# A decoder step on one core: the second layer's pooled products as three fp32r products of halves, 47 to 50 blocks later

## The chip, the cores and the metric

The kernel runs on 1 core of one Trainium2 chip. What is measured is the device time of one execution in microseconds (us); the number given is the median over the runs. Smaller is better. The engines that matter here are TensorE (PE: matmuls and weight loads), VectorE (DVE), ScalarE (ACT), GpSimd (POOL) and SyncE (SP, which issues most DMAs).

## The reference

Two layers of a decoder are computed for 256 prompt rows and 8 sample rows together (T = 264 columns). The second layer has two heads side by side: stick-breaking attention, and a pooling mixer that the change touches. The mixer takes running means of its input `u` over windows of 2, 4, 8 and 16 rows, subtracts `u`, multiplies each of the four 128-wide groups by a 128x128 matrix, and scales the result:

```python
pooled = jnp.concatenate(parts, axis=-1) - u_new.astype(jnp.float32)
pooled = pooled.astype(u_new.dtype).reshape(B, T, POOL_GROUPS, POOL_GROUP_DIM)
mixed = jnp.einsum('btgc,gcd->btgd', pooled, pool_w).reshape(B, T, D_WIDTH)
return mixed * pool_scale
```

Attention output and mixer output are then concatenated and multiplied by `w_out`:

```python
c_out = stick_breaking_attention(q, k_all, v_all, pos).reshape(B, T, C_WIDTH)
d_out = pool_mixer(pool_prev, u, pos, pool_w, pool_scale)
y = jnp.concatenate([c_out, d_out], axis=-1) @ w_out
return x + y, new_kv, new_pool
```

After it come a residual, a feed-forward part with a short convolution, and at the very end a norm.

## The kernel before

**Blocks.** All large weights pass through TensorE as 1472 blocks of 128x128 in a fixed order (`_PHASES`): in0, out0, ff0, dn0 for the first layer, in1, out1, ff1, dn1 for the second. A block is three fp32r matmuls over 264 columns, since each weight and each operand is cut into a high and a low half: high by high, low operand by high weight, high operand by low weight (L329 to L331). The halves of the weights are made eight blocks at a time (a tile): ScalarE writes the high half `wh` (L304), VectorE the low half `wl` (L305), three tiles ahead of use, in four buffers each.

**in1 and out1.** Phase in1 has 128 blocks: blocks 1 to 32 make `u`, 33 to 64 `q`, 65 to 96 `k`, 97 to 128 `v`, eight blocks for each 128 output rows. The accumulators are called after the block number over the whole kernel: `mm848`, `mm856`, `mm864`, `mm872` are the four of `v` (blocks 97, 105, 113 and 121 of in1), `mm880` is the first of out1. out1 starts with its k rows 4 to 7, which are the mixer's output `catB`, before it comes to the attention's output `catA` (`kb` in `_phases`).

**Hooks.** `blk(b, f)` calls f after block b of the phase. In in1 TensorE is held in program order (`fixed[0] = True`), so a hook's matmuls stand exactly after that block. The order on VectorE and ScalarE is made when the program is built, by a scheduler with its own model of times; on the chip each engine then works its list strictly in that order. The hooks of in1 that matter: the pooled sums at 33 (`pool_sum`), the pooled products at 62, 66, 70 and 76 (`pool_mix`), the sample scores at 72 (`zs_score`), the four scores of head pairs at 80, 93, 105 and 117 (`z_qk`, two matmuls each for `Z`; then `stick`: three sigmoids on ScalarE, a scan and a product on VectorE, for each head), and the transposes of `w` and `v` at 117 (`z_tr`, `v_turn`).

**Banks.** PSUM is split into two pools of four banks. The pool `psm` (tag "mm", function `mmb`) gives the banks of the block accumulators, of the pooled products `pm`, and of the transposes `vtp_v` of `v`. Which free bank a new tile takes is settled when the program is built; its first matmul waits until the instruction that empties that bank has run: for `v` that is `v.tensor_tensor(v4[:, t, :], o, R, ALU.mult)` in `in1_evac` (L1098), for `pm` the two instructions that write `catB_h` and `catB_l` (L1088, L1089).

**The pooled product before.** `pool_mix(t)` is one fp32 matmul of 128x128 by 128x264, which the chip runs as two instructions, and the two instructions that scale it and cut it into the halves `catB_h` (ScalarE) and `catB_l` (VectorE).

Of the kernel before, what the change touches and what calls it, by code (L numbers as in the profile page):

```python
# [9 lines left out]
F32 = mybir.dt.float32  # L10
F32R = mybir.dt.float32r
BF16 = mybir.dt.bfloat16
I32 = mybir.dt.int32
AF = mybir.ActivationFunctionType
ALU = mybir.AluOpType
# [3 lines left out]
P = 128  # L19
# [4 lines left out]
T = SEQ + NS  # L24
# [182 lines left out]
def tile_decoder_step(ctx: ExitStack, tc: tile.TileContext, a):  # L207
    nc = tc.nc
    v, s, g = nc.vector, nc.scalar, nc.gpsimd
# [14 lines left out]
    pe = TensorE()  # L224
# [10 lines left out]
    def f4(name, shape=(P, 4, T), dt=F32):  # L235
        return up.tile(list(shape), dt, tag="u", name=name)

    def mv(name):
        return [f4(f"{name}_{x}", (P, 4, TW), F32R) for x in "hl"]
# [4 lines left out]
    def at(name):  # L244
        return psa.tile([P, 512], F32, tag="at", name=name)
# [10 lines left out]
    def mmb(name):  # L256

        return psm.tile([P, 512], F32, tag="mm", name=name)

    def vec(n):  # L260
        o, w = _VEC[n]
        return VEC[:, o:o + w]
# [109 lines left out]
    pw = at("warm")  # L372
# [527 lines left out]
    blk = lambda b, f, *x: hk.at(b / 8 - 1, f, *x)  # L900
# [73 lines left out]
    pw = f4("pw", (P, 4, P))  # L974
# [3 lines left out]
    st1 = {}  # L978
# [82 lines left out]
    pl = f4("pl")  # L1061
# [5 lines left out]
    def pool_sum():  # L1067
# [3 lines left out]
        for t, W in enumerate(POOLW):  # L1071
# [8 lines left out]
            v.tensor_reduce(ss, PALL[:, t, :, 16 - W:16], AX.X, ALU.add)  # L1080
            v.scalar_tensor_tensor(pl[:, t, SEQ:T], ss, 1.0 / W, PALL[:, t, :, NST], ALU.mult, ALU.subtract)

    def pool_mix(t):
        pm = mmb(f"pm{t}")
        pe.matmul(pm[:, :T], pw[:, t, :], pl[:, t, :], start=True, stop=True)
        hh, ll = catB[0][:, t, :T], catB[1][:, t, :T]
        gs = vec("ps")[:, t:t + 1]
        s.activation(hh, pm[:, :T], AF.Copy, scale=gs)  # L1088
        v.scalar_tensor_tensor(ll, pm[:, :T], gs, hh.bitcast(F32), ALU.mult, ALU.subtract)  # L1089
# [12 lines left out]
    blk = lambda b, f, *x: hk.at(b / 8 - 1, f, *x)  # L1102
# [10 lines left out]
    blk(84, late, a["poolp"], plp)  # L1113
    blk(84, late, a["pools"], PALL)
    blk(112, late, a["k1"], k4)
    for i, b in enumerate((62, 66, 70, 76)):
        blk(b, pool_mix, i)
    blk(117, lambda: v_turn(vt, v4, range(0, 2), "v1", mmb))
    blk(107, lambda: sample_av(st1, PZ, vtiles, "l1"))
# [52 lines left out]
    for i, (h, m, e) in enumerate(YD):  # L1172
        n = TG[h][1] - TG[h][0]
        y = f4(f"yo{i}", (P, e - m, n))
        w = r[:, TF:] if i == 2 else ns[h][:, HV[h]]
# [74 lines left out]
```

## Time and profile before

| | |
|---|---|
| median of 3 runs | 591.30 us (591.25 to 591.41) |
| the profiled execution | 591.39 us, of which the span of the core is 589.6 us |
| mean granted TensorE clock | 0.998 |
| TensorE busy in the span | 582.4 us (99%) |
| TensorE weight loads | 567.0 us (96%) |
| VectorE busy | 428.8 us (73%) |
| ScalarE busy | 338.2 us (57%) |
| DMA | 122.42 MB, 208 GB/s on average |

The page divides the span by engine, then in 40 slices, then by DMA queue, then follows the chain of waits back from the last instruction, then groups the instructions. Here the chain is TensorE's to 99%. Matmuls overlap in the pipe, so the duration of one in the trace (0.28 us) is more than its share of the time; the distance from one start to the next is what a matmul costs. in1 lies at 300.5 to 362.6 us, the pooled products at 323.5 to 334 us.

### The profile page before, as it was taken

To read this page: it belongs to the slowest core of one execution; us is meant where nothing else is said; L and a number is where in the kernel's file an instruction comes from. 1 tells how busy PE (TensorE), PEld (TensorE's weight loads), DVE (VectorE), ACT (ScalarE), POOL (GpSimd) and SP (SyncE) were. 2 spreads that over 40 slices of the span, in tenths; PEclk is the share of its full clock that TensorE was granted. 3 is DMA by queue.
4 is the path that set the end of the run, shared out by engine and by line. 5 is a ranking of instruction groups with operands and counts; after the bars stand their busy time and mean duration, and the time that the engine had idled before them with its cause. 6 is when DMAs were issued, how large, how long until landed. Compare 5 with 4: busy or idle time off the path is not lost.

```text
span 589.6 us, 12426 instructions
## 1 busy us (share of the span) xinstructions
PE 582.4 (99%) x4972; PEld 567.0 (96%) x4972; DVE 428.8 (73%) x771; ACT 338.2 (57%) x597; POOL 45.2 (8%) x62
## 2 busy tenths in 40 slices
PE   9999999999999999999999999999999999999995
PEld 8999879999999999999999879999999999999995
DVE  6999876787877877566669675778787777756552
ACT  7749746665655655544454556567565565555431
POOL 1000213200000000011030000120000000002111
PEclk9999999999999999999999999999999999999999
DMA  8998764564545455894558772554554546464501
GB/s 349 408 394 294 248 224 166 187 206 157 210 152 206 163 196 178 314 346 170 199 208 288 240 237 89 182 202 170 190 186 172 200 158 215 149 218 154 205 1 73
DMA packets 27564, 122.42 MB, mean 208 GB/s; under 512 B 3314, under 2 KB 4338, under 8 KB 16114
## 3 DMA queue, kind: packets, MB, share of 16 engines
q1 hardware_dynamic: 27072, 120.75, 57.5%
q8 instruction: 39, 0.64, 0.4%
q10 hardware_dynamic: 434, 0.87, 0.4%
q14 instruction: 19, 0.16, 0.1%
HBM read 117.65 MB, written 3.96 MB: 206 GB/s over the span
## 4 chain that ended last, share of the span: by engine, by line
PE 99%; issue 0%; POOLq 0%; DVE 0%; ACT 0%
PE mm L219 91%; PE sc L219 1%; PE pv_l L219 1%; PE pav L219 1%; PE warm L219 1%; PE Z L219 1%; PE S L219 1%; PE pt L222 1%; PE pf L219 0%; PE pm L219 0%; POOLq L1225 0%; PE vtp_v L222 0%; PE ns_n L219 0%; PE po_l L222 0%; PE vtp_sgu L222 0%
## 5 line engine op out<-in xcount | busy, mean ns | idle before, releaser
L304 ACT ACTIVATE wh<-raw 128x1024 fp32r<-128x1024 f32 x177 | 187.3, 1060 | 197.1 <-PE mm L219 186.3
L305 DVE TENSOR_TENSOR wl<-raw,wh 128x1024 fp32r<-128x1024 f32 x177 | 217.1, 1227 | 104.5 <-ACT wh L304 103.9
L219 PE MATMUL mm<-xg_f_h,wh 128*128 128x264 f32 x704 | 199.9, 284 | 0.0
L219 PE MATMUL mm<-xg_f_h,wl 128*128 128x264 f32 x704 | 199.8, 284 | 0.0
L219 PE MATMUL mm<-xg_f_l,wh 128*128 128x264 f32 x704 | 198.6, 282 | 0.0
L219 PEld LDWEIGHTS mm<-xg_f_l,wh 128*128 128x128 f32 x704 | 132.8, 189 | 0.0
L219 PEld LDWEIGHTS mm<-xg_f_h,wh 128*128 128x128 f32 x704 | 132.5, 188 | 0.0
L219 PEld LDWEIGHTS mm<-xg_f_h,wl 128*128 128x128 f32 x704 | 132.4, 188 | 0.0
L219 PE MATMUL mm<-a_h,wl 128*128 128x264 f32 x352 | 100.0, 284 | 0.0
L219 PE MATMUL mm<-a_h,wh 128*128 128x264 f32 x352 | 100.0, 284 | 0.0
L219 PE MATMUL mm<-a_l,wh 128*128 128x264 f32 x352 | 99.7, 284 | 0.0
L219 PEld LDWEIGHTS mm<-a_l,wh 128*128 128x128 f32 x352 | 66.4, 189 | 0.0
L219 PEld LDWEIGHTS mm<-a_h,wh 128*128 128x128 f32 x352 | 66.2, 188 | 0.0
L219 PEld LDWEIGHTS mm<-a_h,wl 128*128 128x128 f32 x352 | 66.2, 188 | 0.0
L219 PE MATMUL mm<-xg_h,wh 128*128 128x264 f32 x160 | 47.1, 294 | 0.0
L219 PE MATMUL mm<-xg_l,wh 128*128 128x264 f32 x160 | 46.0, 287 | 0.0
L219 PE MATMUL mm<-xg_h,wl 128*128 128x264 f32 x160 | 45.9, 287 | 0.0
L219 PE MATMUL mm<-xg_n_h,wh 128*128 128x264 f32 x128 | 38.0, 297 | 0.0
L219 PE MATMUL mm<-xg_n_h,wl 128*128 128x264 f32 x128 | 36.4, 285 | 0.0
L219 PE MATMUL mm<-xg_n_l,wh 128*128 128x264 f32 x128 | 36.3, 284 | 0.0
L219 PEld LDWEIGHTS mm<-xg_h,wh 128*128 128x128 f32 x160 | 30.6, 191 | 1.5 <-issue 1.2
L219 PEld LDWEIGHTS mm<-xg_l,wh 128*128 128x128 f32 x160 | 30.6, 191 | 0.2 <-DVE xg_l L388 0.2
(261 smaller groups left out, 843.4 us busy)
## 6 DMA issues: line engine op xcount, KB each, us to landing
raw<-in_w SPq DMA_DIRECT2D x89, 1024.0 KB, 4.8
K<-in_kt SPq DMA_DIRECT2D x32, 256.0 KB, 6.4
V<-in_vp SPq DMA_DIRECT2D x32, 256.0 KB, 6.6
raw<-in_w SPq DMA_DIRECT2D x4, 512.0 KB, 6.9
X<-in_x SPq DMA_DIRECT2D x4, 264.0 KB, 6.3
xw<-in_xw SPq DMA_DIRECT2D x2, 388.0 KB, 5.3
out_y<-yo SPq DMA_DIRECT2D x2, 300.0 KB, 2.6
out_k<-k SPq DMA_DIRECT2D x1, 528.0 KB, 6.0
```

The lines of the kernel that those rows point to most:

```text
L219: return self.keep(nc.tensor.matmul(*x, **k))
L222: return self.keep(nc.tensor.transpose(*x, **k))
L304: s.activation(h, src, AF.Copy)
L305: v.tensor_tensor(l, src, h.bitcast(F32), ALU.subtract)
```

## The change

A new hook after block 74, `pool_cut`, cuts the pooled sums `pl` (128 x 4 x 264) and the four matrices `pw` (128 x 512) into high and low halves: two instructions on ScalarE, two on VectorE. `pool_mix` then makes each product by three fp32r matmuls of halves (high by high, low operand, low weight) in place of one fp32 matmul, and its hooks move from blocks 62, 66, 70, 76 to 110, 113, 120, 123. The scaling and cutting of the product is as it was. Three more tiles of the general SBUF pool (24 buffers) are taken, for the halves.

```diff
@@ -1080,9 +1080,19 @@
+    def pool_cut():
+        st1["pw"] = f4("pwr", (P, 2, 4, P), F32R)
+        st1["pl"] = mv("plr")
+        for src, h, l in ((pw, st1["pw"][:, 0], st1["pw"][:, 1]), (pl, *(i[:, :, :T] for i in st1["pl"]))):
+            s.activation(h, src, AF.Copy)
+            v.tensor_tensor(l, src, h.bitcast(F32), ALU.subtract)
+
     def pool_mix(t):
         pm = mmb(f"pm{t}")
-        pe.matmul(pm[:, :T], pw[:, t, :], pl[:, t, :], start=True, stop=True)
+        w = [st1["pw"][:, i, t, :] for i in range(2)]
+        x = [i[:, t, :T] for i in st1["pl"]]
+        for i, j in ((0, 0), (0, 1), (1, 0)):
+            pe.matmul(pm[:, :T], w[i], x[j], start=i + j == 0, stop=i == 1)
         hh, ll = catB[0][:, t, :T], catB[1][:, t, :T]
         gs = vec("ps")[:, t:t + 1]
         s.activation(hh, pm[:, :T], AF.Copy, scale=gs)
@@ -1113,7 +1123,8 @@
     blk(84, late, a["poolp"], plp)
     blk(84, late, a["pools"], PALL)
     blk(112, late, a["k1"], k4)
-    for i, b in enumerate((62, 66, 70, 76)):
+    blk(74, pool_cut)
+    for i, b in enumerate((110, 113, 120, 123)):
         blk(b, pool_mix, i)
     blk(117, lambda: v_turn(vt, v4, range(0, 2), "v1", mmb))
     blk(107, lambda: sample_av(st1, PZ, vtiles, "l1"))
```

**TensorE from block 120 of in1 into out1.** What stands there before: `mm864` is the third accumulator of `v`, `mm872` the fourth, `mm880` the first of out1; a name in brackets is the engine whose count the instruction waits for.

```order
L219 MATMUL mm864_4824<-xg_n11_h_1798,wl108_4637 128x264
L219 MATMUL mm872_4904<-xg_n10_h_1796,wh109_4704 128x264
L219 MATMUL mm872_4904<-xg_n10_l_1797,wh109_4704 128x264
L219 MATMUL mm872_4904<-xg_n10_h_1796,wl109_4705 128x264
...
L219 MATMUL mm880_4938<-catB1_h_4118,wh110_4736 128x264 [waits DVE_49]
L219 MATMUL mm880_4938<-catB1_l_4119,wh110_4736 128x264
```

And in the changed kernel:

```order
L219 MATMUL mm864_4821<-xg_n11_h_1798,wl108_4628 128x264
L219 MATMUL pm2_4901<-plr_h_4536,pwr_4535 128x264 [waits DVE_49]
L219 MATMUL pm2_4901<-plr_l_4537,pwr_4535 128x264
L219 MATMUL pm2_4901<-plr_h_4536,pwr_4535 128x264
L219 MATMUL mm872_4913<-xg_n10_h_1796,wh109_4695 128x264 [waits DVE_49]
L219 MATMUL mm872_4913<-xg_n10_l_1797,wh109_4695 128x264
L219 MATMUL mm872_4913<-xg_n10_h_1796,wl109_4696 128x264
...
L219 MATMUL pm3_4923<-plr_h_4536,pwr_4535 128x264 [waits Activation_49]
...
L219 MATMUL mm880_4953<-catB1_h_4118,wh110_4727 128x264 [waits Activation_49]
L219 MATMUL mm880_4953<-catB1_l_4119,wh110_4727 128x264 [waits DVE_49]
```

The products `pm2` and `pm3` now stand before and inside the blocks of `mm872`. The first matmul of `mm872` had no wait and has one on VectorE; in the built program its count is that of the instruction which empties `mm864` (`v4b<-mm864`). The four banks of the pool explain it: before, `mm864` had bank 2 and `mm872` bank 3; now `pm1` and after it `pm2` have bank 3, the two transposes of `v` banks 1 and 0, and `mm872` follows `mm864` on bank 2. Before, the count of `v4b<-mm864` was waited for by the first matmul of `mm880`, eight blocks later. `pm3` waits for ScalarE, at the copy that empties the first transpose bank (`vt<-vtp_v10_0`). In out1 the first matmuls that read the third product's halves wait for them.

**VectorE over the same stretch.** Before, from the scan of the last head pair on (`keep0` and `keep1` are what is scanned, `w1_6` and `w1_7` the two heads, `v4b` the emptied `v`):

```order
L1002 SCALAR_TENSOR_TENSOR keep0_4127<-keep0_4127,edge_4125 128x383 [waits DVE_49,Activation_49]
L1003 TENSOR_TENSOR w1_6_4846<-w1_6_4846,keep0_4127 128x384 [waits DVE_49,Activation_49]
L1002 SCALAR_TENSOR_TENSOR keep1_4128<-keep1_4128,edge_4125 128x383 [waits Activation_49]
L1003 TENSOR_TENSOR w1_7_4852<-w1_7_4852,keep1_4128 128x384 [waits DVE_49,Activation_49]
L1098 TENSOR_TENSOR v4b_4114<-mm864_4824,R_n1_4222 128x264 [waits PE_49]
L305 TENSOR_TENSOR wl112_4901<-raw59_4634,wh112_4900 128x1024 [waits DMAHW3_49,Activation_49]
L1098 TENSOR_TENSOR v4b_4114<-mm872_4904,R_n1_4222 128x264 [waits PE_49]
L305 TENSOR_TENSOR wl113_4935<-raw59_4634,wh113_4934 128x1024 [waits Activation_49]
```

And in the changed kernel:

```order
L1002 SCALAR_TENSOR_TENSOR keep0_4127<-keep0_4127,edge_4125 128x383 [waits DVE_49,Activation_49]
L1003 TENSOR_TENSOR w1_6_4849<-w1_6_4849,keep0_4127 128x384 [waits DVE_49,Activation_49]
L1002 SCALAR_TENSOR_TENSOR keep1_4128<-keep1_4128,edge_4125 128x383 [waits Activation_49]
L1003 TENSOR_TENSOR w1_7_4855<-w1_7_4855,keep1_4128 128x384 [waits DVE_49,Activation_49]
L1108 TENSOR_TENSOR v4b_4114<-mm864_4821,R_n1_4222 128x264 [waits PE_49]
L305 TENSOR_TENSOR wl112_4910<-raw59_4625,wh112_4909 128x1024 [waits DMAHW3_49,Activation_49]
L1099 SCALAR_TENSOR_TENSOR catB1_l_4119<-pm2_4901,VEC_80,catB1_h_4118 128x264 [waits Activation_49]
L1099 SCALAR_TENSOR_TENSOR catB1_l_4119<-pm3_4923,VEC_80,catB1_h_4118 128x264 [waits Activation_49]
L1108 TENSOR_TENSOR v4b_4114<-mm872_4913,R_n1_4222 128x264 [waits PE_49]
L305 TENSOR_TENSOR wl113_4950<-raw59_4625,wh113_4949 128x1024 [waits Activation_49]
```

The emptying of `mm864` keeps its place behind both scans and both products; the two halves `catB_l` of the third and fourth product stand behind the low half `wl112` of a weight tile. Elsewhere on VectorE and ScalarE the four pairs for `catB` are gone from between the tiles at blocks 62 to 76, and `pool_cut`'s two instructions stand on each engine ahead of those of the sample scores.

## Rows read from the trace of the kernel before

**Rows 1.** Section 1 of the page: engine, busy us (share), instructions

```profile
PE 582.4 (99%) x4972; PEld 567.0 (96%) x4972; DVE 428.8 (73%) x771; ACT 338.2 (57%) x597; POOL 45.2 (8%) x62
```

**Rows 2.** The table of waits, TensorE alone, whole span: us, times, longest

```profile
PE warm L219 <- DVE warm L371: 1.2, 1, 1.2
```

**Rows 3.** Timeline of TensorE at the first pooled product: start us, us, engine, line, instruction

```profile
323.33 0.28 PE L219 MATMUL mm<-xg_n_h,wl 128*128 128x264 f32 x1
323.46 0.61 PE L219 MATMUL pm<-pl,pw 128*128 128x264 f32 x2
323.71 0.48 PE L219 MATMUL mm<-xg_n_h,wh 128*128 128x264 f32 x1
324.02 0.28 PE L219 MATMUL mm<-xg_n_l,wh 128*128 128x264 f32 x1
324.15 0.28 PE L219 MATMUL mm<-xg_n_h,wl 128*128 128x264 f32 x1
```

**Rows 4.** Timeline of TensorE from the last head pair to out1

```profile
357.06 0.93 PE L219 MATMUL Z<-k4b,q4b 64*128 64x128 f32 x8
...
358.54 0.39 PE L219 MATMUL mm<-xg_n_h,wh 128*128 128x264 f32 x1
...
359.73 0.28 PE L219 MATMUL mm<-xg_n_h,wh 128*128 128x264 f32 x1
...
362.62 0.28 PE L219 MATMUL mm<-catB_h,wh 128*128 128x264 f32 x1
...
363.47 0.28 PE L219 MATMUL mm<-catB_l,wh 128*128 128x264 f32 x1
```

**Rows 5.** Timeline of VectorE over the same stretch, idle time before in brackets

```profile
358.65 0.96 DVE L1002 TENSOR_TENSOR_SCAN keep<-keep,edge 128x383 f32<-128x383 f32 x1 [1.12 <-ACT keep L1000]
...
361.72 0.42 DVE L1098 TENSOR_TENSOR v4b<-mm,R_n 128x264 f32<-128x264 f32 x1
363.55 1.23 DVE L305 TENSOR_TENSOR wl<-raw,wh 128x1024 fp32r<-128x1024 f32 x1 [1.41 <-ACT wh L304]
364.69 0.43 DVE L1098 TENSOR_TENSOR v4b<-mm,R_n 128x264 f32<-128x264 f32 x1
```

**Rows 6.** Timeline of ScalarE over the same stretch

```profile
358.07 0.55 ACT L1000 ACTIVATE keep<-Z 128x127 f32<-128x127 f32 x2 [1.79 <-PE Z L219]
...
361.90 0.67 ACT L550 ACTIVATE vt<-vtp_v 128x256 f32<-128x256 f32 x2
362.43 2.03 ACT L304 ACTIVATE wh<-raw 128x1024 fp32r<-128x1024 f32 x2
```

**Rows 7.** All instructions on the products' banks: ns smallest, median, largest

```profile
L1088 ACT ACTIVATE catB_h<-pm,VEC x4: 482/483/484, 324.1 to 334.3; 128x264 fp32r<-128x264 f32 x4
L1089 DVE SCALAR_TENSOR_TENSOR catB_l<-pm,VEC,catB_h x4: 492/492/495, 324.6 to 334.8; 128x264 fp32r<-128x264 f32 x4
```

**Rows 8.** Timeline of ScalarE and VectorE where the new hook falls

```profile
328.51 1.06 ACT L304 ACTIVATE wh<-raw 128x1024 fp32r<-128x1024 f32 x1
332.26 0.39 ACT L1009 ACTIVATE keep_s<-sc 128x256 f32<-128x256 f32 x1 [2.69 <-PE sc L219]
...
329.60 1.23 DVE L305 TENSOR_TENSOR wl<-raw,wh 128x1024 fp32r<-128x1024 f32 x1 [0.35 <-ACT wh L304]
332.67 0.69 DVE L1011 TENSOR_TENSOR_SCAN keep_s<-keep_s,edge 128x256 f32<-128x256 f32 x1 [1.85 <-ACT keep_s L1009]
```

**Rows 9.** Timeline of TensorE near the start

```profile
6.90 0.41 PE L219 MATMUL mm<-xg_l,wh 128*128 128x264 f32 x1
7.12 0.32 PE L219 MATMUL mm<-xg_h,wl 128*128 128x264 f32 x1
```

**Rows 10.** Three stretches near the end: length, busy by engine (count), granted clock, DMA

```profile
583.00:584.00 1.00, 0.64 (x3) 0.30 (x2) 0.72 (x2) 0.78 (x3) 0.00 (x0) 1.00 0.00 0
586.00:587.00 1.00, 0.00 (x0) 0.00 (x0) 0.00 (x0) 0.00 (x0) 0.00 (x0) 1.00 0.93 360
587.50:588.00 0.50, 0.00 (x0) 0.00 (x0) 0.00 (x0) 0.00 (x0) 0.00 (x0) 0.50 0.96 373
```

## The prediction

> **What bounds the kernel now.** I read the page's engine table first: TensorE is busy for 582.4 of 589.6 us [rows 1]. Then the table of waits for TensorE: in the whole span there is one wait, 1.2 us before the first matmul [rows 2]. So every matmul that goes is a gain, every one added a loss, and any wait put into TensorE's list is paid in full, for no slack behind it can take it up. What VectorE and ScalarE do costs nothing as long as TensorE needn't wait. The third view is the timeline of TensorE where the change works, the fourth those of VectorE and ScalarE over the same stretch.
>
> **The matmuls removed.** Ordinary matmuls start 0.12 us apart. From 323.33 to 324.02 there stand two such steps and one fp32 product [rows 3], so the product took 0.69 - 0.24 = 0.45 us. Four: 1.80 us. (The product's own durations overlap with its neighbours and say less.)
>
> **The matmuls added.** Twelve fp32r matmuls of the same shape as a block's. From 359.73 to 362.62 there are 24 of those in 2.89 us [rows 4], 0.120 us each, so 0.36 per product and 1.45 in all. The direct gain is 1.80 - 1.45 = 0.35 us.
>
> The Trainium skill (FP8 and Floating Point Precision, TensorE Precision Notes) says that true fp32 makes four passes through the array; three passes for four would then save a quarter, 0.45 of 1.80 us, against 0.35 by the rows, which count the step between matmuls too.
>
> **The cutting hook.** `pool_cut` adds on ScalarE a 128x512 and a 128x1056 copy; the nearest row, a cut of 128x1024, takes 1.06 us [rows 8], so some 0.55 and 1.1, together 1.6 us. They fall between a weight tile and the sample scores' first sigmoid, where ScalarE is idle for 2.69 us. On VectorE the nearest row is 1.23 us for 128x1024, so 0.6 and 1.27, about 1.9 us, where it is idle for 1.85 us before the scan [rows 8]. The scan may start 0.1 us late; TensorE reads its result some 3 us later. Cost nothing. If the cover were gone the scan would be 1.9 us late, still ahead of the transposes that read it after block 82. The four scalings (0.48 us on ScalarE, 0.49 on VectorE each [rows 7]) are the same, only elsewhere.
>
> **The new wait.** This is what decides. The first matmul of `mm872`, block 121, now waits until VectorE has emptied `mm864`; before, the first matmul of out1 did, eight blocks later. The list of VectorE holds that instruction behind two scans and two products for the last head pair, which hang on that pair's `Z`. Counting from the start of `Z` (357.06):
> - the emptying ends at 361.72 + 0.42 = 362.14 [rows 4, 5], 5.08 us after `Z`;
> - block 121 starts at 359.73 [rows 4], 2.67 us after `Z`. In the changed kernel `pm2` stands ahead of it, so TensorE is ready 2.67 + 0.36 = 3.03 us after `Z`;
> - from the end of one engine's instruction to the start of the one released, a row shows 329.60 - (328.51 + 1.06) = 0.03 us [rows 8].
>
> The wait is 5.08 + 0.03 - 3.03 = 2.08 us. Before, out1 started at 362.62, 0.48 us after the emptying: it just missed a wait. Does the chain from `Z` to the emptying change? ScalarE is idle for 1.79 us before its first sigmoid and VectorE for 1.12 us before the scan [rows 5, 6]; into this idle time come `catB` of `pm0` and `pm1`, of which the last `catB_l` (0.49 us) stands behind a weight tile's low half. It fits: VectorE's next waits for ScalarE, and ScalarE's for `Z`. The chain keeps its 5.08 us. Bounds for the wait: none if the emptying came in time, and 2.08 + 0.5 if the extra `catB_l` delayed the scan by its whole length. I take 2.08.
>
> **What is late next.** While TensorE waits, ScalarE empties the transposes of `v` (by 362.57 [rows 6]; in the changed kernel 1.07 us earlier, since its `Z` starts after two new products in place of four old ones, 1.80 - 0.73). `pm3` needs the first of those, at about 361.2; after the wait TensorE reaches it at 362.2. In out1 the second matmul of the third block reads `catB_l` of `pm2`. VectorE makes it after `wl112`, which runs 363.55 to 364.69 [rows 5]; 1.07 earlier, plus 0.49, is 364.1. TensorE gets there after the wait at about 365.2 (363.47 [rows 4], -0.35 +2.08). So neither adds anything. Without the wait at block 121 they would: TensorE would reach that matmul at 363.1 and stand for 1.0 us.
>
> **The sum.** 591.39 (the profiled execution) - 1.80 + 1.45 + 2.08 = 593.12 us. The median shown is 0.09 lower, so 593.0 against 591.30: slower by 0.3%. 0.2%, or 1.2 us, is about what a measurement of this kernel can tell from no change.
>
> **The rivals.**
> - *Not slower: the bank is free in time.* If VectorE's emptying came before block 121, only the wait for `catB_l` in out1 would be left, 1.0 us, hence 591.30 - 0.35 + 1.0 = 592.0, within 0.2%; if its scaling were also early, 590.95, which is within 0.2% too. It turns on the row of `v4b` for `mm864` ending before TensorE is done with `pm2`. For it: VectorE has 1.41 us idle right behind that row and 1.12 before the scans [rows 5]. Against it: the list's order is fixed, and each scan needs its sigmoid, which needs `Z`. For the chain to shrink by 2 of its 5.08 us I see no reason. Chance 0.10.
> - *The wait is longer.* The moved scalings stand in the lists of both engines. Should they delay a sigmoid or a scan of the last pair, the emptying slips by the same time: 0.5 us for one, 1.0 for both halves of `pm1`. 593.5 to 594.0. Against it stand the two idle times above. Chance 0.10.
> - *The clock falls.* Near the start matmuls stood 0.22 us apart, up to the one at 7.12 us, against 0.12 later [rows 3, 9]: about the lower of the two clocks (1.2 and 2.4 GHz), until 5.9 us after the first matmul at 1.2 [rows 2]. Near the end the granted clock was full for over 2 us after the last matmul had ended (0.64 of the stretch 583 to 584 was busy), and 0.50 from 587.5 on [rows 10]. If the 2.08 us of waiting brought it down for as long as at the start, it would cost 5.9 x 0.1/0.22 = 2.7 us more: 595.7. [...] The rows at the end show full clock in the stretch 586 to 587, over 2 us into a gap, which speaks against it here. Chance 0.05.
> - *The change doesn't do what it says*, the fp32r products costing as much as the fp32 ones: 593.4, inside the range.
>
> **How the numbers follow.** The forecast, 592.5 to 593.5, has 0.75, the longer wait 0.10, the bank in time 0.10, the fallen clock 0.05. Range 592.3 to 594.1: the forecast, the longer wait, and the uncertainty of 0.2 of the readings. Slower by over 0.2% (above 592.5): 0.75 and 0.10 and 0.05, less 0.04 for a forecast that ends just under the mark, 0.86. Within 0.2%: 0.13. Faster by over 0.2% (below 590.1) needs more than the whole direct gain: 0.01.
>
> **What would show it.** In the trace of the changed kernel: one wait of about 2.1 us on TensorE at the first matmul behind `pm2`, put down to VectorE's `v4b`; the fp32r products at 0.12 us steps; no gap at the old places; ScalarE and VectorE filled between the weight tile and the sample scores; no wait at the start of out1; the clock full throughout. I am wrong if that wait is missing or under 1.5 us, or if TensorE waits somewhere else that I have costed at nothing.

## The result: 594.64 us, slower by 0.5%, and the profile after

The changed kernel takes 594.64 us (median of 6 runs, 593.35 to 594.97), the kernel before 591.27 us (median of 6 runs, 591.24 to 591.41). The ratio is 1.0053 with a 95% interval of 1.0043 to 1.0063: slower by 3.37 us, where the prediction had 1.7 us. (A ratio here is an estimate over all runs, with its interval, and need not be the quotient of the two medians.) The profiled execution took 594.45 us with a span of 592.7 us.

The engine table of the page and the table of waits of TensorE in the changed kernel, which answer to [rows 1, 2]:

```profile
PE 583.5 (98%) x4976; PEld 568.2 (96%) x4976; DVE 431.0 (73%) x773; ACT 339.5 (57%) x599; POOL 45.2 (8%) x62
```

```profile
PE mm L219 <- DVE v4b L1108: 1.9, 1, 1.9
PE warm L219 <- DVE warm L371: 1.2, 1, 1.2
```

TensorE's busy time rose by 1.1 us, though it has less to do. The forecast wait is there, once, at the forecast instruction, and there is no other. Yet the wait (2.10 us, below) less the gain of the products (0.35) explains only half of the 3.4 us. The timeline of TensorE through the place, which answers to [rows 4], shows the rest:

```profile
355.65 0.93 PE L219 MATMUL Z<-k4b,q4b 64*128 64x128 f32 x8
...
358.32 0.28 PE L219 MATMUL pm<-plr_h,pwr 128*128 128x264 f32 x1
358.45 0.28 PE L219 MATMUL pm<-plr_l,pwr 128*128 128x264 f32 x1
358.57 0.28 PE L219 MATMUL pm<-plr_h,pwr 128*128 128x264 f32 x1
360.79 0.41 PE L219 MATMUL mm<-xg_n_h,wh 128*128 128x264 f32 x1 [1.94 <-DVE v4b L1108]
361.01 0.40 PE L219 MATMUL mm<-xg_n_l,wh 128*128 128x264 f32 x1
361.22 0.42 PE L219 MATMUL mm<-xg_n_h,wl 128*128 128x264 f32 x1
...
364.30 0.35 PE L219 MATMUL mm<-xg_n_l,wh 128*128 128x264 f32 x1
364.49 0.28 PE L219 MATMUL mm<-xg_n_h,wl 128*128 128x264 f32 x1
...
365.69 0.28 PE L219 MATMUL mm<-catB_h,wh 128*128 128x264 f32 x1
```

From 358.57 to 360.79 there are 2.22 us in which one step of 0.12 would have done: the wait is 2.10 us (the bracket gives 1.94 because it counts from the modelled end of the last matmul). Behind it the starts are 0.22 us apart instead of 0.12, for 17 steps, up to 364.49: 3.70 us where 17 x 0.120 = 2.05 us had been. These 1.65 us are the part that was not forecast. 0.10 of them is the first step, from 360.79 to 361.01: such a step takes as long behind a stand at full clock (361.10 to 361.33 in the kernel with the new places and the old products, below). The other 16 steps cost 1.55 us more than at 0.12. The granted clock says why; each row is a stretch, its length, the busy time of each engine with its count of instructions, the granted clock, and the DMA's share and rate:

```profile
358.80:360.70 1.90, 0.05 (x1) 0.00 (x0) 1.80 (x4) 1.89 (x4) 0.00 (x0) 1.00 0.58 241
360.80:361.00 0.20, 0.20 (x1) 0.20 (x2) 0.00 (x0) 0.20 (x2) 0.00 (x0) 1.00 0.00 0
361.00:362.00 1.00, 1.00 (x6) 1.00 (x6) 0.00 (x0) 1.00 (x3) 0.00 (x0) 0.51 0.00 0
362.00:363.00 1.00, 1.00 (x7) 1.00 (x6) 0.87 (x1) 0.47 (x2) 0.00 (x0) 0.50 0.08 16
363.00:364.00 1.00, 1.00 (x6) 1.00 (x6) 0.76 (x2) 0.34 (x1) 0.00 (x0) 0.50 0.00 0
364.00:365.00 1.00, 1.00 (x9) 1.00 (x8) 0.49 (x1) 0.14 (x1) 0.00 (x0) 0.78 0.00 0
365.00:366.00 1.00, 1.00 (x11) 1.00 (x10) 0.10 (x1) 0.23 (x1) 0.00 (x0) 1.00 0.00 0
```

The clock was full while TensorE stood and for the first 0.2 us after it had begun again; then it was at its lower level, 1.2 GHz, for about 3.4 us of unbroken work. This is easy to miss: no wait is listed for these steps, TensorE is "busy" all the time, and in the 40 slices the place is one 8 among 9s in the clock's row (the other 8 there is the last slice).

The ledger closes on the first matmul of out1. It starts at 365.69, and before at 362.62 [rows 4], 3.07 us later: 1.45 - 1.80 for the products, +2.10 for the wait, +0.10 for the first step behind it, +1.55 for the half clock, and -0.33 because this execution was already 0.33 us ahead at `Z` (355.65 against 357.06: 1.41 earlier, of which four old products less the two new ones that stand ahead of `Z`, 1.80 - 0.72 = 1.08, are the change's). That last term arose ahead of in1, which began at 300.13 against 300.49; over the ten traces it began at 300.13 to 300.56. From out1's start to the end of the span both have 227.0 us.

The rest is as forecast. On VectorE, which answers to [rows 5], the chain behind `Z` is as it was:

```profile
357.24 0.96 DVE L1002 TENSOR_TENSOR_SCAN keep<-keep,edge 128x383 f32<-128x383 f32 x1 [1.06 <-ACT keep L1000]
...
360.31 0.43 DVE L1108 TENSOR_TENSOR v4b<-mm,R_n 128x264 f32<-128x264 f32 x1
...
363.27 0.49 DVE L1099 SCALAR_TENSOR_TENSOR catB_l<-pm,VEC,catB_h 128x264 fp32r<-128x264 f32 x1
```

And where the cutting hook falls, the timeline of ScalarE, then that of VectorE, for [rows 8]:

```profile
327.83 0.61 ACT L1087 ACTIVATE pwr<-pw 128x512 fp32r<-128x512 f32 x1
328.35 1.07 ACT L1087 ACTIVATE plr_h<-pl 128x1056 fp32r<-128x1056 f32 x1
330.60 0.38 ACT L1009 ACTIVATE keep_s<-sc 128x256 f32<-128x256 f32 x1 [1.19 <-PE sc L219]
```

```profile
329.09 0.69 DVE L1088 TENSOR_TENSOR pwr<-pw,pwr 128x512 fp32r<-128x512 f32 x1
329.70 1.25 DVE L1088 TENSOR_TENSOR plr_l<-pl,plr_h 128x1056 fp32r<-128x1056 f32 x1
331.02 0.69 DVE L1011 TENSOR_TENSOR_SCAN keep_s<-keep_s,edge 128x256 f32<-128x256 f32 x1
```

ScalarE still idles for 1.19 us behind its two, VectorE's scan comes right behind its two; no wait of TensorE follows from either.

### The profile page after: what moved, and what is told of

Its sections match the earlier page's. It is cut to its first block, busy times and chain, and to the rows that moved or that the text cites. A ratio compares the mean times of both kernels' runs of the same rounds, so it can differ in the third digit from the quotient of the medians.

```text
span 592.7 us, 12440 instructions
## 1 busy us (share of the span) xinstructions
PE 583.5 (98%) x4976; PEld 568.2 (96%) x4976; DVE 431.0 (73%) x773; ACT 339.5 (57%) x599; POOL 45.2 (8%) x62
## 4 chain that ended last, share of the span: by engine, by line
PE 98%; issue 1%; DVE 1%; POOLq 0%; ACT 0%; DVEq 0%
PE mm L219 91%; PE sc L219 1%; PE pv_l L219 1%; PE pav L219 1%; PE warm L219 1%; PE S L219 1%; PE pt L222 0%; PE Z L219 0%; DVE keep L1002 0%; PE pf L219 0%; PE pm L219 0%; POOLq L1236 0%; PE vtp_v L222 0%; PE ns_n L219 0%; DVE w L1003 0%
```

## The experiments

Theory A: the wait is the forecast one, and the rest is TensorE's clock, which falls because TensorE stands for 2.1 us. Theory B: the half clock comes with something else of the change (the cut halves, the products' new place) or is there whatever TensorE did before. The four kernels up to "Earlier places" ran on one chip, where the kernel before took 591.19 us (16 runs, 590.99 to 591.46), the rest on another, where it took 591.27 us (22 runs, 591.06 to 591.57). The changed kernel itself was measured on neither occasion: its 594.64 us stand beside 591.27 us for the kernel before, 3.37 us less.

**TensorE kept busy through the wait.** The changed kernel with 17 products behind `pm2` that nothing reads, on a free bank of the other pool.

```diff
+    def pad(n):
+        p, x = at("pad"), st1["pl"][0][:, 0, :T]
+        for i in range(n):
+            pe.matmul(p[:, :T], st1["pw"][:, 0, 0, :], x, start=i == 0, stop=i == n - 1)
...
+    blk(120, pad, 17)
```

> The changed kernel, with 17 more matmuls (128x128 by 128x264, fp32r, results unused, into a free bank) on TensorE between the third product and the matmul that waits. They take 17 x 0.12 = 2.04 us, all inside the wait of 2.1 us, so they add nothing themselves. Theory A (the wait lets TensorE's clock fall, and the matmuls behind it run at the lower level for 3.7 us): with the array busy the clock stays, 594.6 - 1.65 = 593.0 us, and no steps of 0.22 us behind the place. Theory B (the 1.6 us beyond the wait come from somewhere else): 594.6 us as before.

Measured: 593.16 us (6 runs, 592.91 to 593.34), 1.0034 [1.0021, 1.0046]. More work made the kernel 1.5 us faster. The timeline of TensorE:

```profile
358.70 0.28 PE L219 MATMUL pm<-plr_h,pwr 128*128 128x264 f32 x1
358.83 2.20 PE L219 MATMUL pad<-plr_h,pwr 128*128 128x264 f32 x17
360.93 0.39 PE L219 MATMUL mm<-xg_n_h,wh 128*128 128x264 f32 x1
361.15 0.28 PE L219 MATMUL mm<-xg_n_l,wh 128*128 128x264 f32 x1
```

The distance from `pm2` to the next block is the same (2.23 us); the steps behind it are 0.12 us. The granted clock of the same kernel in the three stretches that were at half:

```profile
361.00:362.00 1.00, 1.00 (x10) 1.00 (x9) 0.00 (x0) 1.00 (x3) 0.00 (x0) 1.00 0.08 16
362.00:363.00 1.00, 1.00 (x11) 1.00 (x10) 0.73 (x1) 0.92 (x3) 0.00 (x0) 1.00 0.00 0
363.00:364.00 1.00, 1.00 (x11) 1.00 (x10) 1.00 (x3) 0.17 (x1) 0.00 (x0) 1.00 0.00 0
```

So here the fall hangs on TensorE's standing still, and its price is the 1.5 us between the two kernels (1.4 us when each is taken against the kernel before that was measured beside it: 3.37 less 1.97).

**The wait alone.** The kernel before, with one unused matmul on a bank of the accumulators' pool behind block 120 and a one-column copy on ScalarE that empties it, which pushes `mm872` onto `mm864`'s bank. Nothing of the change is in it.

```diff
+    def hold(n):
+        for i in range(n):
+            p = mmb(f"hold{i}")
+            pe.matmul(p[:, :T], onesr, xg[0][0][:, 0, :T], start=True, stop=True)
+            s.activation(sm.tile([P, 1], F32, tag="hold", name=f"h{i}", bufs=2), p[:, :1], AF.Copy)
...
+    blk(120, hold, 1)
```

> The kernel before, products as they were, plus one extra matmul (128x264, result unused) into a new bank of the same pool after block 120, so that the fourth accumulator of v takes the third one's bank: the wait alone, without fp32r products. It adds 362.14 + 0.03 - 359.73 = 2.44 us. Theory A: the clock falls too, 591.3 + 2.4 + 1.65 = 595.4 us. Theory B: 593.7 us.

Measured: 595.43 us (5 runs: four at 595.28 to 595.69, one at 593.72), 1.0065 [1.0051, 1.0078]. The timeline of TensorE, and one stretch of the granted clock:

```profile
359.80 0.28 PE L219 MATMUL hold<-xg_n_h,onesr 128*128 128x264 f32 x1
362.27 0.59 PE L219 MATMUL mm<-xg_n_h,wh 128*128 128x264 f32 x1 [2.19 <-DVE v4b L1104]
362.65 0.42 PE L219 MATMUL mm<-xg_n_l,wh 128*128 128x264 f32 x1
```

```profile
363.00:364.00 1.00, 1.00 (x7) 1.00 (x6) 0.40 (x1) 0.64 (x2) 0.00 (x0) 0.50 0.00 0
```

A taken bank is enough for the whole loss, wait and half clock, with the fp32 products where they were. The one run at 593.72 fits the wait without the fall (the extra matmul 0.12, the wait 362.27 - 359.80 - 0.12 = 2.35: 591.19 + 0.12 + 2.35 = 593.66).

**The new places with the old products.** The kernel before, its four fp32 products moved to blocks 110, 113, 120 and 123.

```diff
-    for i, b in enumerate((62, 66, 70, 76)):
+    for i, b in enumerate((110, 113, 120, 123)):
```

> The kernel before with its fp32 products moved to blocks 110, 113, 120 and 123, nothing cut: the move alone. TensorE comes to the wait 3.12 us after Z, so it waits 1.99 us. Theory A: 591.3 + 2.0 + 1.65 = 594.9 us, with 0.22 us steps behind the wait. Theory B, if what is beyond the wait hangs on the fp32r products: 593.3 us.

Measured: 593.53 us (5 runs: 593.37, 593.42, 593.53, and 594.94, 595.07), 1.0051 [1.0038, 1.0065]. The median lies near the number of theory B, but the runs fall into two cases, and two of the five are at the number of theory A with the fp32 products in place: the median decides nothing here. The profiled one, of 593.37 us, is one without the fall:

```profile
358.63 0.61 PE L219 MATMUL pm<-pl,pw 128*128 128x264 f32 x2
361.10 0.39 PE L219 MATMUL mm<-xg_n_h,wh 128*128 128x264 f32 x1 [1.85 <-DVE v4b L1098]
361.33 0.28 PE L219 MATMUL mm<-xg_n_l,wh 128*128 128x264 f32 x1
```

The wait belongs to the new places, not to the products' form. Behind it the first step is 0.23 us and the next are 0.12, the clock being full. And the fall isn't certain at 1.85 us of standing: two runs of five.

**Earlier places.** The changed kernel with the products behind blocks 84, 86, 88 and 90, to take the wait away.

```diff
-    for i, b in enumerate((110, 113, 120, 123)):
+    for i, b in enumerate((84, 86, 88, 90)):
```

> The changed kernel with the three-matmul products at blocks 84, 86, 88 and 90 in place of 110, 113, 120 and 123; the accumulators of v then get back their old banks and nobody waits. Both theories: only the direct gain of 0.35 us is left, 590.9 us, faster than before by 0.06%. If the cutting hook cost something on the path it would be slower than 591.3.

Measured: 591.35 us (11 runs, 591.19 to 591.64), 1.0003 [0.9994, 1.0012]: the loss is gone, but 0.4 us is missing from what was expected. A new, smaller gap stands behind the third product. TensorE, then VectorE:

```profile
338.81 0.28 PE L219 MATMUL pm<-plr_h,pwr 128*128 128x264 f32 x1
339.21 0.39 PE L219 MATMUL mm<-xg_n_h,wh 128*128 128x264 f32 x1
```

```profile
336.04 1.79 DVE L1002 TENSOR_TENSOR_SCAN keep<-keep,edge 128x383 f32<-128x383 f32 x2
...
338.67 0.88 DVE L1099 SCALAR_TENSOR_TENSOR catB_l<-pm,VEC,catB_h 128x264 fp32r<-128x264 f32 x2
```

It is the same fault in small: the bank of a product is emptied behind the scans of a head pair, here the first. The gap is 339.21 - 338.81 - 0.12 = 0.28 us, and the first step behind it, 0.23 us to 339.44, is 0.11 longer than usual: together 0.39 of the 0.4 us. TensorE's table of waits doesn't list it; that of its weight loads does, with the cause:

```profile
PEld mm L219 <- DVE catB_l L1099: 0.3, 1, 0.3
```

**Shorter standing.** The first experiment's kernel with 3 and with 7 products in place of 17. After the kernels above, theory B is here that any wait at this place brings the fall, however short it is.

> The changed kernel with 3 unused products (128x128 by 264, fp32r, 0.12 us each) behind the third pooled product: TensorE then stands about 2.10 - 0.36 = 1.7 us at the wait for v4b instead of 2.1, and the wait ends at the same moment. Theory A (the clock falls because TensorE stands, and less often the shorter it stands): runs without a fall at 593.1, fewer of them at 594.7 than the 5 of 6 of the changed kernel, so about the 2 of 5 of the run with 1.85 us or fewer; median 593.2. Theory B (any wait at this place brings the fall, whatever its length): 594.6 as in the changed kernel.

> The same with 7 unused products: TensorE stands about 2.10 - 0.84 = 1.3 us. Theory A: no fall in any run, 593.1 in all. Theory B: 594.6.

Measured: 593.26 us (5 runs, 593.23 to 593.51) and 593.25 us (6 runs, 593.19 to 593.62), both 1.0035 (intervals 1.0021 to 1.0049 and 1.0023 to 1.0047). The rows of the wait, of the kernel with 3 and of the one with 7:

```profile
361.12 0.39 PE L219 MATMUL mm<-xg_n_h,wh 128*128 128x264 f32 x1 [1.57 <-DVE v4b L1113]
```

```profile
361.05 0.39 PE L219 MATMUL mm<-xg_n_h,wh 128*128 128x264 f32 x1 [1.09 <-DVE v4b L1113]
```

The wait is still there, at the same place and for the same bank; by their times none of 11 runs lost the second part. So neither the place, nor the bank, nor the halves bring the fall by themselves, and theory B falls in both of its forms. Three useless products, 0.36 us of TensorE's time, were worth 1.4 us (3.37 less 1.99 over the kernel before), at no cost, since they stand inside the wait.

**Another bank.** The changed kernel with `pm2` in the other pool of PSUM.

```diff
-        pm = mmb(f"pm{t}")
+        pm = (at if t == 2 else mmb)(f"pm{t}")
```

> The changed kernel with the third pooled product's sum in the other PSUM pool: the first matmul of mm872 then needs a bank that was cleared long before, and the fourth pooled product is the one whose bank waits for v4b of mm864. TensorE comes to it about 1.1 us later than it came to mm872, so 2.1 - 1.1 = 1.0 us of wait is left, and the clock stays full. Theory A (the cost is the standing time plus a fall that needs the long one): about 592.1, without a row at half clock. Rival (the wait only moves and stays whole): 593.1 or more.

Measured: 592.15 us (11 runs, 592.04 to 592.32), 1.0014 [1.0005, 1.0023]. TensorE:

```profile
360.06 0.28 PE L219 MATMUL mm<-xg_n_h,wl 128*128 128x264 f32 x1
361.20 0.39 PE L219 MATMUL pm<-plr_h,pwr 128*128 128x264 f32 x1 [0.85 <-DVE v4b L1108]
```

The gap is 361.20 - 360.06 - 0.12 = 1.02 us, at `pm3`, as expected, and the clock stays full:

```profile
361.00:362.00 1.00, 0.80 (x6) 0.81 (x7) 0.14 (x1) 1.00 (x4) 0.00 (x0) 1.00 0.00 0
```

One bank changed takes 2.5 us off the changed kernel's time. The Trainium skill (Perfetto Trace Analysis, Optimizing Tensor Performance, Matmuls) advises that independent groups of matmuls rotate through different banks, so that one bank is emptied while the next group's matmuls run; the trace agrees, the wait listed for `v4b` being 0.85 us here against 1.94.

**Places without a wait.** The changed kernel with the cut behind block 70 and the products where before had its fourth.

```diff
-    blk(74, pool_cut)
-    for i, b in enumerate((110, 113, 120, 123)):
+    blk(70, pool_cut)
+    for i, b in enumerate((75, 76, 78, 79)):
```

> The changed kernel with the split behind block 70 and the four products behind blocks 75, 76, 78 and 79, where before had its fourth. If the twelve fp32r products cost 0.12 each against 0.45 for each of the four, and no wait is added, 591.2 - 0.35 = 590.9. If the split's work on VectorE and ScalarE makes a wait here (as it did with the products behind 84 to 90, 0.3 us), 591.2.

Measured: 590.95 us (11 runs, 590.84 to 591.28), 0.9996 [0.9987, 1.0005]. The table of waits of TensorE's matmuls lists only the one that was always there:

```profile
PE warm L219 <- DVE warm L371: 1.2, 1, 1.2
```

The medians differ by 0.32 us where 0.35 was expected, but the interval holds 1: that the cheaper products gain anything is not shown by the times, only by the steps in the trace. This is the best version found, and its gain, some 0.05%, is below what can be told.

## Why the prediction was wrong

- **Matmuls removed and added: right.** The twelve new products start 0.12 us apart (358.32, 358.45, 358.57), 0.36 us each. The version without the wait came out 0.32 us faster in the median, for 0.35 in the sum, though its interval holds 1.
- **The cutting hook: right.** 0.61 and 1.07 us on ScalarE (0.55 and 1.1 forecast), 0.69 and 1.25 on VectorE (0.6 and 1.27), in the idle time that was named, at no cost.
- **The new wait: right in place, cause and size.** 2.10 us against 2.08; the sum only lacked the longer first step behind a stand, 0.10 us. The chain from `Z` to the end of the emptying is 360.31 + 0.43 - 355.65 = 5.09 us against 5.08.
- **What is late next: right.** No wait at `pm3` nor at out1. (`wl112` ends at 363.55 + 1.23 = 364.78 [rows 5]; the 364.69 in the working is the start of the next instruction. The 0.09 us change nothing.)
- **The clock: wrong, and the step that failed.** The fallen clock was named as a rival, at a chance of 0.05, on the ground that the stretch 586 to 587 showed "full clock ..., over 2 us into a gap, which speaks against it here" [rows 10]. That row is one gap of one execution, and its clock fell 3.8 us after the last matmul. It showed that a clock *can* stay full that long, and was read as if it always did. The fall that the change brought came about 2.2 us after the last matmul's end (358.57 + 0.28 to some 361.0). At the end of the same execution it took 3.0 us (586.71 to 589.71), and at the end of the kernel with 3 extra products 1.6 us (585.51 to 587.10); the rows of the one, then of the other:

```profile
586.00:586.70 0.70, 0.70 (x4) 0.31 (x3) 0.36 (x1) 0.50 (x3) 0.00 (x0) 1.00 0.00 0
...
589.50:589.75 0.25, 0.00 (x0) 0.00 (x0) 0.00 (x0) 0.00 (x0) 0.00 (x0) 0.92 1.11 403
589.75:590.00 0.25, 0.00 (x0) 0.00 (x0) 0.00 (x0) 0.00 (x0) 0.00 (x0) 0.50 0.94 365
```

```profile
584.52 0.99 PE L219 MATMUL ns_end<-fin,ones 128*128 128x64 f32 x4
587.00:587.25 0.25, 0.00 (x0) 0.00 (x0) 0.25 (x2) 0.00 (x0) 0.25 (x1) 0.69 0.70 279
```

Over the ends of all ten traces it took 1.6, 1.7, 2.0, 2.3, 3.0, 3.1, 3.2 and three times 3.8 us, so the row that the chance was taken from shows one of the longest. The sum held nothing for the fall. A stand of 2.1 us, to which the prediction gave one chance in twenty, brought the fall in 5 of the changed kernel's 6 runs. The Trainium skill (TensorE: Matmul & The Clock Gate, Why this matters for your kernels) warns of idle gaps between bursts of matmuls, but of longer ones than this; where they differ the trace decides, with 0.51 granted behind a stand listed as 1.94 us.

- **The price of the fall: too high in the rival.** 2.7 us was taken from the steps of 0.22 us at the start of the run, though the granted clock of that trace reads 1.00 in every stretch from 0 to 8 us, the row of 6 to 7 us for one, so it stays open whether the clock made them:

```profile
6.00:7.00 1.00, 1.00 (x6) 1.00 (x6) 0.47 (x2) 0.81 (x2) 0.00 (x0) 1.00 1.02 403
```

The half clock here lasted 3.4 us and cost 1.55 us (16 steps), 1.4 to 1.5 by the kernel that fills the gap. With this and the first step behind the wait the sum is 591.27 - 0.35 + 2.10 + 0.10 + 1.55 = 594.67; measured 594.64.

- **The range** held only the runs without the fall: the changed kernel had one such in six, at 593.35.

What stays open is why one execution of a program falls and the next doesn't. The runs count the cases: with 1.85 us or more of standing in the brackets 11 of 16 (2 of 5 at 1.85, 5 of 6 at 1.94, 4 of 5 at 2.19), with 1.57 us or less none of 22. For the runs without a trace the case is told by the time; the granted clock of the whole run agrees in the three kernels that show both cases, 0.994 to 0.996 in the eleven long runs and 0.997 or 0.998 in the five short ones.

## What to carry to other kernels

A wait on a busy TensorE has two prices, the time it stands and the half clock that may follow. Look for the second in the granted clock and in the steps between starts behind the gap, for the table of waits has only the first; and where a wait of some 2 us can't be avoided, try putting work into it, even useless work: here it gave back 1.4 us. Before moving a small product between blocks, ask which bank its accumulator takes from whom: a few small products moved into a new stretch gave an untouched block another bank, and that block then waited for an instruction that stood in VectorE's list behind two scans and two products and ended 5.09 us after the scores they hang on. That something held once for so long is no bound for when it gives way: look at the same place in every trace at hand, and price a rival for which one row is all the evidence with that in mind.

## What the hardware showed that was not expected

- The clock could fall after TensorE was already back at work: in the changed kernel it was full at 360.80 to 361.00 with TensorE busy, and 0.51 in the next stretch, for 3.4 us of dense matmuls. In the kernel with the wait alone it fell at about 362.2, just ahead of the first matmul at 362.27.
- The time from the last matmul's end to the fall differed from trace to trace, 1.6 to 3.8 us at the ends of ten.
- The first step behind a stand was 0.22 or 0.23 us in place of 0.12 at full clock too (361.10 to 361.33 with the old products in the new places; 0.22 or 0.23 in the kernels with shorter standing and with another bank).
- The same program shows two times, by whether this happens: 594.45 to 594.97 and 593.35 in the changed kernel, and 1.3, 1.6 and 1.8 us between the medians of the two groups in the three kernels that show both.
